# A hybrid decoder layer: two-input elementwise work of the token mixers moved from GpSimd to VectorE and ScalarE

## The chip, the cores and the metric

The kernel runs on one core of a Trainium2 chip. The metric is the device time of one execution in microseconds; the number compared is the median of several runs. Engines are named as in the profile: PE (TensorE, matmuls), PEld (its weight loads), DVE (VectorE), ACT (ScalarE), POOL (GpSimd) and SP (the queue that issues most DMAs).

## The reference, cut to what matters

One layer, 256 tokens by 1024 features, float32. All projections of the token mixers come from one product, then two mixers run side by side, and a sparse expert network follows.

```python
proj = h @ w_in                       # 1024 x 7184
xa, ga, q, k, v, go, glr, ma, mb = split(proj)
xa = causal_depthwise_conv(xa)        # 4 taps
ya = rg_lru(xa) * gelu(ga)            # a = exp(-s); h = a h + sqrt(1 - a^2) * i * x  along the tokens
log_g = log_sigmoid(glr @ w_gate + b) / 16
o  = gla(q, k, v, log_g)              # gated linear attention, 4 heads
yb = o * rsqrt(mean(o^2) + eps) * norm_g * silu(go)
y  = sigmoid(ma) * ya + sigmoid(mb) * yb
h  = layer_norm(alpha * h + y @ w_out)
h  = layer_norm(alpha * h + moe(h))   # top 4 of 32 experts: every expert's weights are read
h  = h + sigmoid(h @ w_ple_gate + b) * (p @ w_ple)
```

## The kernel before

The order of the work is written out by hand: every engine runs its instructions in the order in which the code issues them, and there is no scheduler. Two large parts follow each other.

**The mixers.** The projection is done in blocks of 128 output channels (`proj(n, b)`; for `v` blocks of tokens, `vblock`). Each block's weights, a "half" of 128x1024, come from a DMA and are split into a high and a low part so that three passes of matmuls give a nearly exact float32 product: ACT copies the high part (L268), and L269 subtracts it to get the low part. A block is 24 matmuls of 256 columns. `split` runs up to four halves ahead (`NW = 4`), in the order xa, q, k, v, ma, ga, go, mb, wo, 64 halves in all. The table `ONPOOL` says which of them have L269 on POOL; the others have it on DVE.

The list `seq` gives the order of the blocks (8 of xa, 4 of q, 4 of k, 8 of v, 8 of ma, 8 of ga, 8 of go), and the table `hooks` says which pieces of the mixers' own work are issued behind which block: the recurrence (`lru_*`), and the attention, whose decayed products are built in levels 0 to 7. For a level, `lvl_sub` makes two halves of exponents (L467, L468), `lvl_exp` takes exp of them on ACT (L471), `lvl_mul` multiplies one half by the keys and the other by the queries (L477, L478), and `lvl` multiplies them on PE ("gr" in the profile) and puts the result in place (L496, L503, L508). Levels 0 to 5 are used early; level 7's matmuls (L507) stand ahead of the second ga block, and `assemble` and `gla_out` come after them.

The blocks of `mb` come last, with a loop of engines around each (`ev_mb`): a sigmoid on ACT (L616), two DVE products (L617, L618), ACT's high part of the result (L620), DVE's low part (L621). The halves split in that loop are the later ones of mb and the first of wo. Then `y_out` multiplies by w_out.

**The experts.** All 32 experts' weights, 12.6 MB each, stream from HBM through the large buffers that the mixers give back (`Slots`, 22 tiles of 8 KB a partition; `Stream.pump` issues the next load on SP as soon as a buffer is free). Each expert is 32 matmuls up and 16 down of 512 columns at full float32. Behind them come the second norm and the gated embedding.

Of the kernel before, what the change touches and what calls it, by code (L numbers as in the profile page):

```python
# [13 lines left out]
AF = mybir.ActivationFunctionType  # L14
# [14 lines left out]
class Slots:  # L29
    """The large buffers: tiles of 8 KB a partition that change hands. keep of them stay free for takes to come."""  # L30
# [17 lines left out]
class Stream:  # L48
    """Large loads in a fixed order, each issued as soon as a buffer is free for it."""
# [24 lines left out]
    def give(self, *names, keep=0):  # L74
        """Buffers back, keep of them for takes to come."""
        self.slots.keep += keep
        for name in names:
            self.slots.free.append(self.slots.held.pop(name))
        self.pump()
# [3 lines left out]
def hybrid_layer(ctx, tc, x, p, w_in, conv_w, conv_b, lru_w_r, lru_b_r, lru_w_i, lru_b_i, lru_lambda,  # L83
# [64 lines left out]
    # buffers held at the start, and those that the mixers take later: six of the split weights, the LRU's and the GLA's  # L148
# [66 lines left out]
    # integer level masks of the scores: entry (j, i) belongs to level l when (i ^ j) >> l == 1 and i > j  # L215
# [26 lines left out]
    # ================= phase 1: token mixers =================  # L242
    # ---- exact splits of float32 operands in two parts of 12 bits, and their products in three passes
    HALVES = [(key, c) for key in PIECES for c in range(2)]
    W3, lru = {}, {}
    ONPOOL = (1, 2, 5, 6, 12, 14, 26, 32, 35, 36, 42, 47, 48, 52, 53, 54, 55, 57, 63, 65, 70)
    ahead = {"next": 0, "keep": NW}

    def w_keep():
        """Buffers kept for the halves to split next."""  # L250
        n = min(NW - len(W3), len(HALVES) - ahead["next"])
        hold(n - ahead["keep"])
        ahead["keep"] = n

    def split(m, n=1):
        """High and low parts of the halves of pieces up to half m, as far as the buffers for them go; each in n steps."""
# [22 lines left out]
    def mm3(o, l, r, ks, first=True, last=True):  # L279
        """o += sum over k of l(k).T @ r(k), each a pair (high, low): high x high, high x low, low x high."""  # L280
# [21 lines left out]
    # four blocks of channels each: first mixer's output; recurrence gate, then second mixer's output  # L302
# [13 lines left out]
    yb = rr  # L316
# [17 lines left out]
    def lru_decay():  # L334
        """4 * softplus(-lambda), the logarithm of 1 + u as 2 * artanh(u / (2 + u)); the gates' sigmoids come as (tanh + 1) / 2."""
# [29 lines left out]
    def glr():  # L365
        """Low-rank decay gate."""
# [4 lines left out]
    def decay1():  # L371
        """Logarithms of the decays (times 16) and their running sums."""
# [33 lines left out]
    # ---- the projection's blocks of 128 channels, with the mixers' work in between  # L406
    xc, QK = {}, {}

    def proj(n, b):
        """Channel-major block b of projection n: psum [128 channels, 256 tokens]."""  # L410
# [8 lines left out]
    def conv(b, o):  # L419
        t = xc[b] = aa[:, b]  # L420
        V.tensor_scalar(t, o, pc("cw", 24 + b), pc("cb", b), op0=OP.mult, op1=OP.add)
# [3 lines left out]
    def lru_gates(b):  # L425
# [6 lines left out]
        G.tensor_scalar(ix[:, b, :], ix[:, b, :], 1.0, None, op0=OP.add)  # L432
        G.tensor_tensor(ix[:, b, :], ix[:, b, :], t, op=OP.mult)
# [5 lines left out]
    def lru_sq(h):  # L439
        G.tensor_tensor(ya(h, 4), aa[:, h:h + 4], aa[:, h:h + 4], op=OP.mult)  # L440

    def lru_one(h):
        """1 - a^2 as tanh(s) * (1 + a^2) with a = exp(-s)."""
        V.scalar_tensor_tensor(rr(h, 4), ya(h, 4), 1.0, rr(h, 4), op0=OP.add, op1=OP.mult)

    def lru_sqrt(h):
        A.activation(rr(h, 4), rr(h, 4), AF.Sqrt, scale=0.25)
# [13 lines left out]
    # level lv of the decayed products: queries of the right, keys of the left half of each 2s tokens,  # L461
    # both scaled by the decay to the last token of the left half
    def lvl_sub(lv):
# [3 lines left out]
        G.tensor_tensor(half(d, 0, s), ref, half(bc, 0, s), op=OP.subtract)  # L467
# [5 lines left out]
    def lvl_mul(lv):  # L473
# [3 lines left out]
        G.tensor_tensor(half(k2, 0, s), half(d, 0, s), half(kT, 0, s), op=OP.mult)  # L477
# [50 lines left out]
    def split_bu(n):  # L528
        """Biases of the experts in three exact bfloat16 parts, stacked on the partitions."""
# [8 lines left out]
    def router_prep():  # L538
        """Norm's scale and shift folded into the router: scaled weights, their column sums, and the bias, on all partitions."""
# [17 lines left out]
    def gla_out(h):  # L557
# [6 lines left out]
        V.tensor_copy(yb(2 * h, 2), o)  # L564
        G.tensor_tensor(sqs[h], yb(2 * h, 2), yb(2 * h, 2), op=OP.mult)

    def gla_ms(h):
        """Mean squares of a head, tokens on the partitions."""
# [22 lines left out]
    def ev_q(b, o):  # L591
        V.tensor_scalar(qT[:, b, :], o, 128.0 ** -0.5, None, op0=OP.mult)

    def ev_k(b, o):
        V.tensor_copy(kT[:, b, :], o)

    def ev_ga(b, o):
        gl = tmp("gl", p1, 3)
        A.activation(gl, o, AF.Gelu_apprx_tanh)
        G.tensor_tensor(ya(b), ya(b), gl, op=OP.mult)  # L600

    def ev_go(b, o):
# [3 lines left out]
        G.tensor_tensor(yb(b), yb(b), sg, op=OP.mult)  # L606

    def ev_ma(b, o):
        sg = tmp("sg", p1, 3)
        A.activation(sg, o, AF.Tanh, scale=0.5)  # L610
        G.tensor_scalar(sg, sg, 0.5, 0.5, op0=OP.mult, op1=OP.add)
        G.tensor_tensor(ya(b), ya(b), sg, op=OP.mult)
# [24 lines left out]
    def swap(*names):  # L637
        """Buffers back, kept for as many takes to come."""
        give(*names, keep=len(names))

    # what runs after each piece, by the piece's number
# [80 lines left out]
    # ================= routing =================  # L722
# [5 lines left out]
    def ln_scale(sb, name):  # L728
        """1/std and -mean/std of the rows of both token tiles."""
# [9 lines left out]
    # residual and its transpose; the norm is applied to the logits, while the tokens are normalized beside  # L739
# [33 lines left out]
    def up_start(sel):  # L773
        """Gate and up pre-activations, tokens x d_ff: the halves of d_ff lie on the two halves of the partitions."""
# [492 lines left out]
```

## Time and profile before

| | us |
|---|---|
| median of 3 runs | 1234.04 |
| the runs | 1232.08 to 1234.21 |
| span of the profiled execution, first to last instruction | 1230.1 |
| median less span | 3.9 |

| engine | busy us in the span | share |
|---|---|---|
| PE | 1152.5 | 94% |
| DVE | 421.5 | 34% |
| ACT | 246.1 | 20% |
| POOL | 176.4 | 14% |

The profiled execution's own time is known by its span; the 3.9 us are what the runs' median has more, before the first and after the last instruction. Shares over the whole span mix the mixers (roughly the first 257 us) with the experts, in which DVE, ACT and POOL have little to do, so the sections below go by stretches. A busy PE is not PE at its peak, since the ends of matmuls are modelled.

### The profile page before, as it was taken

Reading aid. Unit: us, or ns where it says so; the run is one execution under the profiler, and the core shown is the slowest. Engines: PE = TensorE matmul, PEld = TensorE weight load, DVE = VectorE, ACT = ScalarE, POOL = GpSimd, SP = SyncE. Lnnn points to the kernel's source line nnn. Section 1 sums busy time; section 2 is a strip of 40 time slices with the busy share of each in tenths; the row PEclk is TensorE's granted clock in tenths of the full one; section 3 lists DMA queues with packets and bytes.
Section 4 is the critical chain, followed back from the end, with each engine's and each line's share of the span. In section 5 each row is a group of like instructions: output and inputs, shape, how many; then the busy total and the mean of one; then the engine's idle time right before and its main releaser. Section 6 shows DMA issues by size and latency. Waiting matters only on the chain.

```text
span 1230.1 us, 14483 instructions
## 1 busy us (share of the span) xinstructions
PE 1152.5 (94%) x5930; PEld 570.8 (46%) x5930; DVE 421.5 (34%) x680; ACT 246.1 (20%) x390; POOL 176.4 (14%) x149
## 2 busy tenths in 40 slices
PE   7998799889999999999999999899889989999987
PEld 7998799654433334333433433243234323433336
DVE  7699566731121222222121221212121212121248
ACT  4674454421111001000100100010001000200043
POOL 5757854210000000000000000000000000000025
PEclk9999899999999999899999999999999999999999
DMA  9653647588989999999999999999999999999960
GB/s 320 208 172 103 203 167 308 209 339 347 426 330 426 426 427 427 419 426 428 426 427 427 426 427 426 427 426 426 427 426 427 427 426 426 426 428 427 426 287 35
DMA packets 92715, 447.07 MB, mean 363 GB/s; under 512 B 9258, under 2 KB 40336, under 8 KB 43397
## 3 DMA queue, kind: packets, MB, share of 16 engines
q1 hardware_dynamic: 91040, 444.72, 88.2%
q10 hardware_dynamic: 1364, 1.10, 0.4%
q8 instruction: 48, 0.79, 0.2%
q0 software_dynamic: 240, 0.28, 0.1%
q14 instruction: 23, 0.18, 0.0%
HBM read 445.03 MB, written 1.05 MB: 363 GB/s over the span
## 4 chain that ended last, share of the span: by engine, by line
PE 56%; DMA 29%; DVE 7%; POOL 3%; issue 2%; ACT 2%; ACTq 0%; DVEq 0%; SPq 0%; POOLq 0%
PE gu L860 22%; DMA up<-in_w_up_dram 18%; PE dn L887 12%; DMA dn<-in_w_down_dram 11%; PE pj L283 6%; PE ga L840 4%; PE sc L920 2%; PE g L851 1%; PE acc L283 1%; PE pg L1136 1%; DVE sg L617 1%; PE gu L778 1%; DVE sgt L906 1%; PE aTp L879 1%; PE bc L929 1%
## 5 line engine op out<-in xcount | busy, mean ns | idle before, releaser
L860 PE MATMUL gu<-up,xe 128*64 128x512 f32 x1792 | 415.7, 601 | 16.6 <-DMA up<-in_w_up_dram 15.9
L860 PEld LDWEIGHTS gu<-up,xe 128*64 128x64 f32 x1792 | 121.4, 137 | 264.5 <-issue 207.4
L887 PE MATMUL dn<-dn,mo 128*64 128x512 f32 x1024 | 228.8, 597 | 5.0 <-DMA dn<-in_w_down_dram 4.8
L896 DVE COPY y2b<-dn 64x512 f32<-64x512 f32 x32 | 22.2, 694 | 379.0 <-ACT mo L898 369.2
L887 PEld LDWEIGHTS dn<-dn,mo 128*64 128x64 f32 x1024 | 73.2, 138 | 155.2 <-issue 142.1
L957 POOL DMA_DIRECT2D pp<-in_p_dram x1 | 0.8, 845 | 754.9 <-DMA up<-in_w_up_dram 754.9
L867 DVE TENSOR_SCALAR mo<-gu 128x512 f32<-128x512 f32 x32 | 22.1, 692 | 184.4 <-PE gu L860 184.4
L898 ACT ACTIVATE mo<-dn 64x512 f32<-64x512 f32 x32 | 18.9, 592 | 268.3 <-PE dn L887 268.3
L868 ACT ACTIVATE mo<-mo 128x512 f32<-128x512 f32 x32 | 20.2, 631 | 226.2 <-DVE mo L867 226.2
L860 PE MATMUL gu<-up,x 128*64 128x512 f32 x256 | 62.6, 613 | 0.0
L880 ACT ACTIVATE mo<-aTp 128x512 f32<-128x512 f32 x32 | 19.1, 598 | 206.6 <-PE aTp L879 206.6
L924 DVE TENSOR_TENSOR z<-z,sc 128x512 f32<-128x512 f32 x60 | 41.2, 688 | 48.5 <-PE sc L920 48.5
L840 PE MATMUL ga<-oh,X 128*128 128x256 f32 x224 | 55.1, 389 | 0.0
L840 PEld LDWEIGHTS ga<-oh,X 128*128 128x128 f32 x224 | 40.7, 191 | 21.4 <-DVE mo L867 5.7
L1085 POOL TENSOR_TENSOR pgl<-pg,pgh 128x1024 fp32r<-128x1024 f32 x6 | 16.3, 2748 | 175.4 <-ACT pgh L1084 171.9
L920 PE MATMUL sc<-mo,se 128*128 128x512 f32 x64 | 36.0, 645 | 0.7 <-ACT mo L898 0.7
L845 DVE TENSOR_SCALAR xe<-ga,parTB 128x256 f32<-128x256 f32 x28 | 15.2, 543 | 54.0 <-PE ga L840 54.0
L920 PE MATMUL sc<-y2b,se 128*128 128x512 f32 x64 | 32.7, 592 | 0.0
L843 ACT ACTIVATE xe<-ga,parTB 128x256 f32<-128x256 f32 x28 | 15.8, 565 | 74.8 <-PE ga L840 73.5
L879 PEld LDWEIGHTS aTp<-ident,mo 128*128 128x128 f32 x128 | 18.9, 204 | 20.8 <-issue 16.5
L860 PEld LDWEIGHTS gu<-up,x 128*64 128x64 f32 x256 | 16.3, 139 | 24.5 <-issue 22.4
L851 PEld LDWEIGHTS g<-oh,X 128*128 128x128 f32 x128 | 16.5, 193 | 18.1 <-issue 15.7
(337 smaller groups left out, 1362.9 us busy)
## 6 DMA issues: line engine op xcount, KB each, us to landing
up<-in_w_up_dram SPq DMA_DIRECT2D x256, 1024.0 KB
dn<-in_w_down_dram SPq DMA_DIRECT2D x128, 1024.0 KB
v<-in_w_in_dram SPq DMA_DIRECT2D x4, 1024.0 KB
ma<-in_w_in_dram SPq DMA_DIRECT2D x4, 1024.0 KB
ga<-in_w_in_dram SPq DMA_DIRECT2D x4, 1024.0 KB
go<-in_w_in_dram SPq DMA_DIRECT2D x4, 1024.0 KB
mb<-in_w_in_dram SPq DMA_DIRECT2D x4, 1024.0 KB
wo<-in_w_out_dram SPq DMA_DIRECT2D x4, 1024.0 KB
```

The costliest lines, as they stand in the source:

```text
L283: PE.matmul(o, lhsT=l(k)[i], rhs=r(k)[j], start=first and m == 0, stop=last and m == len(n) - 1)
L840: PE.matmul(o, lhsT=X[:, t, k * 128:(k + 1) * 128], rhs=oh[:, t], start=(t == 0), stop=(t == 1))
L851: PE.matmul(o, lhsT=X[:, t, k * 128:(k + 1) * 128], rhs=oh[:, t, i], start=(t == 0), stop=(t == 1))
L860: PE.matmul(gu[a][64 * hf:64 * hf + 64, :], lhsT=xk, rhs=w[:, (a - parts[0]) * 1024 + hf * 512:(a - parts[0]) * 1024 + hf * 512 + 512], st ...
L867: V.tensor_scalar(gc, gu[0], LIM, None, op0=OP.min)
L868: A.activation(sg, gc, AF.Sigmoid, scale=1.702)
L879: PE.transpose(o[:, q, :], act[:, c * 256 + j:(c + 1) * 256:2], ident)
L880: A.activation(aT, o, AF.Copy)
L887: PE.matmul(o[64 * dh:64 * dh + 64, :], lhsT=aT[:, 2 * c + j, hf * 64:hf * 64 + 64], rhs=w[:, j - js[0], dh * 512:(dh + 1) * 512], start=( ...
L896: V.tensor_copy(dst, src)
L920: PE.matmul(o, lhsT=se[rows, t * 128:(t + 1) * 128], rhs=(y2b if dh else mo[:, 3])[rows], start=True, stop=True)
L924: V.tensor_tensor(z[:, t, dh * 512:(dh + 1) * 512], z[:, t, dh * 512:(dh + 1) * 512], o, op=OP.add)
```

## The change

Nearly all of POOL's two-input work in the mixers goes to DVE or ACT. The table `ONPOOL` keeps two early halves; products that took two instructions on POOL become one `scalar_tensor_tensor` on DVE; squares, the evictions of q, k and of the attention's output, and the first tap of the convolution go to ACT. The factor 0.5 that `ev_ma` drops is taken up by the scale of `lru_sqrt`. The changed file has blank lines in place of comments, and some of its line numbers are lower by one.

```diff
-    ONPOOL = (1, 2, 5, 6, 12, 14, 26, 32, 35, 36, 42, 47, 48, 52, 53, 54, 55, 57, 63, 65, 70)
+    ONPOOL = (1, 2)
...
     def conv(b, o):
         t = xc[b] = aa[:, b]
-        V.tensor_scalar(t, o, pc("cw", 24 + b), pc("cb", b), op0=OP.mult, op1=OP.add)
+        A.activation(t, o, AF.Identity, scale=pc("cw", 24 + b), bias=pc("cb", b))
...
-        G.tensor_scalar(ix[:, b, :], ix[:, b, :], 1.0, None, op0=OP.add)
-        G.tensor_tensor(ix[:, b, :], ix[:, b, :], t, op=OP.mult)
+        V.scalar_tensor_tensor(ix[:, b, :], ix[:, b, :], 1.0, t, op0=OP.add, op1=OP.mult)
...
     def lru_sq(h):
-        G.tensor_tensor(ya(h, 4), aa[:, h:h + 4], aa[:, h:h + 4], op=OP.mult)
+        A.activation(ya(h, 4), aa[:, h:h + 4], AF.Square)
...
-        A.activation(rr(h, 4), rr(h, 4), AF.Sqrt, scale=0.25)
+        A.activation(rr(h, 4), rr(h, 4), AF.Sqrt, scale=0.0625)
...
-        G.tensor_tensor(half(d, 0, s), ref, half(bc, 0, s), op=OP.subtract)
+        V.tensor_tensor(half(d, 0, s), ref, half(bc, 0, s), op=OP.subtract)
...
-        G.tensor_tensor(half(k2, 0, s), half(d, 0, s), half(kT, 0, s), op=OP.mult)
+        V.tensor_tensor(half(k2, 0, s), half(d, 0, s), half(kT, 0, s), op=OP.mult)
...
-        V.tensor_copy(yb(2 * h, 2), o)
-        G.tensor_tensor(sqs[h], yb(2 * h, 2), yb(2 * h, 2), op=OP.mult)
+        A.activation(sqs[h], o, AF.Square)
+        A.activation(yb(2 * h, 2), o, AF.Copy)
...
     def ev_q(b, o):
-        V.tensor_scalar(qT[:, b, :], o, 128.0 ** -0.5, None, op0=OP.mult)
+        A.activation(qT[:, b, :], o, AF.Copy, scale=128.0 ** -0.5)
 
     def ev_k(b, o):
-        V.tensor_copy(kT[:, b, :], o)
+        A.activation(kT[:, b, :], o, AF.Copy)
...
         A.activation(gl, o, AF.Gelu_apprx_tanh)
-        G.tensor_tensor(ya(b), ya(b), gl, op=OP.mult)
+        V.tensor_tensor(ya(b), ya(b), gl, op=OP.mult)
...
         V.tensor_tensor(sg, sg, o, op=OP.mult)
-        G.tensor_tensor(yb(b), yb(b), sg, op=OP.mult)
+        V.tensor_tensor(yb(b), yb(b), sg, op=OP.mult)
...
         A.activation(sg, o, AF.Tanh, scale=0.5)
-        G.tensor_scalar(sg, sg, 0.5, 0.5, op0=OP.mult, op1=OP.add)
-        G.tensor_tensor(ya(b), ya(b), sg, op=OP.mult)
+        V.scalar_tensor_tensor(ya(b), sg, 1.0, ya(b), op0=OP.add, op1=OP.mult)
```

Three places in the queues. First DVE in the v blocks, from the exponents of level 1 to the split of the last v half: "y" and "aa" belong to the recurrence, "gd", "gc", "gq" and "gk" to the levels. Before:

```order
L468 TENSOR_TENSOR gd<-gc 128x256x2
L490 TENSOR_TENSOR gc<-gr,eye_96 128x512
L450 TENSOR_TENSOR y_210<-y_210,ix 128x1024
L454 SCALAR_TENSOR_TENSOR y_210<-aa,y_210 128x256 x4
L450 TENSOR_TENSOR y_211<-y_211,ix 128x1024
L478 TENSOR_TENSOR gq<-gd,gk 128x512
L478 TENSOR_TENSOR gq<-gd,gk 128x256x2
L269 TENSOR_TENSOR v_1047<-v_505,v_1047 128x1024
L269 TENSOR_TENSOR v_1050<-v_505,v_1050 128x1024
```

And with the change:

```order
L467 TENSOR_TENSOR gd<-gc 128x256x2
L468 TENSOR_TENSOR gd<-gc 128x256x2
L490 TENSOR_TENSOR gc<-gr,eye_96 128x512
L450 TENSOR_TENSOR y_210<-y_210,ix 128x1024
L454 SCALAR_TENSOR_TENSOR y_210<-aa,y_210 128x256 x4
L450 TENSOR_TENSOR y_211<-y_211,ix 128x1024
L477 TENSOR_TENSOR gq<-gd,gk 128x512
L478 TENSOR_TENSOR gq<-gd,gk 128x512
L477 TENSOR_TENSOR gq<-gd,gk 128x256x2
L478 TENSOR_TENSOR gq<-gd,gk 128x256x2
L269 TENSOR_TENSOR v_1039<-v_502,v_1039 128x1024
L269 TENSOR_TENSOR v_1042<-v_502,v_1042 128x1024
```

Each level's L467 and L477, which stood in POOL's queue, now stand in DVE's, so both halves of a level are done one after the other.

Second, ACT between the k blocks and the v blocks (L592 and L595 are the evictions of q and k, L439 is the square that was POOL's). Before, from the split of the second k half:

```order
L268 ACTIVATE k_676<-k_140 128x1024
L268 ACTIVATE k_707<-k_205 128x1024
L436 ACTIVATE aa<-y_210,nlam 128x256
L437 ACTIVATE y_210<-y_210,lamc 128x256
L436 ACTIVATE aa<-y_210,nlam 128x256
L437 ACTIVATE y_210<-y_210,lamc 128x256
L268 ACTIVATE k_741<-k_205 128x1024
```

And with the change:

```order
L268 ACTIVATE k_669<-k_140 128x1024
L592 ACTIVATE gk<-pj 128x256
L268 ACTIVATE k_700<-k_205 128x1024
L592 ACTIVATE gk<-pj 128x256
L435 ACTIVATE aa<-y_210,nlam 128x256
L436 ACTIVATE y_210<-y_210,lamc 128x256
L435 ACTIVATE aa<-y_210,nlam 128x256
L436 ACTIVATE y_210<-y_210,lamc 128x256
L439 ACTIVATE y_210<-aa 128x1024
L268 ACTIVATE k_734<-k_205 128x1024
```

Evictions and the square now stand between the high parts that PE and DVE wait for.

Third, DVE around the mb blocks. Before, two blocks in a row, whose splits are on POOL:

```order
L617 TENSOR_TENSOR sg<-sg,y_210 128x256
L618 TENSOR_TENSOR sg<-sg,y_210 128x256
L621 TENSOR_TENSOR yhl<-sg,yhl 128x256
L617 TENSOR_TENSOR sg<-sg,y_210 128x256
L618 TENSOR_TENSOR sg<-sg,y_210 128x256
L621 TENSOR_TENSOR yhl<-sg,yhl 128x256
```

And with the change:

```order
L616 TENSOR_TENSOR sg<-sg,y_210 128x256
L617 TENSOR_TENSOR sg<-sg,y_210 128x256
L620 TENSOR_TENSOR yhl<-sg,yhl 128x256
L269 TENSOR_TENSOR mb_2255<-mb_1620,mb_2255 128x1024
L616 TENSOR_TENSOR sg<-sg,y_210 128x256
L617 TENSOR_TENSOR sg<-sg,y_210 128x256
L620 TENSOR_TENSOR yhl<-sg,yhl 128x256
```

The split of the half that is to come stands in DVE's queue ahead of the block's own products.

## Rows read from the trace of the kernel before

**Rows 1.** Busy time (and instructions) of each engine by stretch, clock, DMA share.

```profile
95.00:111.00 16.00, 14.43 (x199) 13.86 (x195) 15.90 (x17) 5.37 (x8) 10.54 (x7) 0.91 0.25 72
111.00:141.00 30.00, 23.11 (x237) 22.64 (x237) 23.03 (x17) 15.77 (x22) 29.26 (x24) 0.96 0.65 199
141.00:150.00 9.00, 9.00 (x66) 8.88 (x65) 4.22 (x4) 2.91 (x4) 5.87 (x4) 0.74 0.32 92
150.00:204.00 54.00, 54.00 (x430) 53.08 (x428) 31.33 (x40) 28.48 (x37) 31.75 (x24) 1.00 0.68 260
266.00:380.00 114.00, 113.11 (x544) 48.28 (x544) 25.66 (x59) 15.99 (x32) 0.00 (x0) 0.99 0.90 361
380.00:669.00 289.00, 282.79 (x1241) 103.14 (x1242) 69.79 (x125) 26.41 (x46) 0.00 (x0) 0.98 1.01 426
669.00:1173.00 504.00, 473.63 (x2040) 168.53 (x2036) 103.33 (x183) 48.22 (x84) 0.84 (x1) 0.99 1.01 427
```

**Rows 2.** The chain that ended last, one piece from the experts.

```profile
669.23 19.48 DMA up<-in_w_up_dram
```

**Rows 3.** Timeline of mb blocks: start, us, engine, line, [idle before <-releaser].

```profile
219.22 2.39 POOL L269 TENSOR_TENSOR mb<-mb,mb 128x1024 fp32r<-128x1024 f32 x1 [2.21 <-ACT mb L268]
219.44 2.44 DVE L617 TENSOR_TENSOR sg<-sg,y 128x256 f32<-128x256 f32 x1 [0.79 <-ACT sg L616]
...
222.71 1.04 ACT L268 ACTIVATE mb<-mb 128x1024 fp32r<-128x1024 f32 x1
...
227.31 1.04 ACT L268 ACTIVATE wo<-wo 128x1024 fp32r<-128x1024 f32 x1
...
228.39 1.23 DVE L269 TENSOR_TENSOR wo<-wo,wo 128x1024 fp32r<-128x1024 f32 x1 [0.52 <-ACT wo L268]
...
229.53 0.42 DVE L617 TENSOR_TENSOR sg<-sg,y 128x256 f32<-128x256 f32 x1
...
230.76 1.05 ACT L268 ACTIVATE wo<-wo 128x1024 fp32r<-128x1024 f32 x1
```

**Rows 4.** PE in the timeline of the v, ma and first ga blocks.

```profile
94.57 3.56 PE L484 MATMUL gr<-gq 128*64 128x64 f32 x64 [2.83 <-DVE gq L478]
...
140.60 1.97 PE L501 MATMUL gr<-gq 128*64 128x64 f32 x16 [6.89 <-POOL gq L477]
...
142.50 2.08 PE L283 MATMUL pj<-xh,ga 128*128 128x256 f32 x8
...
146.84 1.05 PE L507 MATMUL gr<-gq 128*128 128x128 f32 x8
...
147.65 1.20 PE L283 MATMUL pj<-xh,ga 128*128 128x256 f32 x8
```

**Rows 5.** DVE in the same stretch, timeline.

```profile
92.62 1.20 DVE L450 TENSOR_TENSOR y<-y,ix 128x1024 f32<-128x1024 f32 x1
93.74 1.28 DVE L478 TENSOR_TENSOR gq<-gd,gk 128x512 f32<-128x512 f32 x2
94.94 4.04 DVE L269 TENSOR_TENSOR v<-v,v 128x1024 fp32r<-128x1024 f32 x2
...
100.11 3.47 DVE L454 TENSOR_TENSOR_SCAN y<-aa,y 128x256 f32<-128x256 f32 x4
...
129.76 0.74 DVE L496 COPY_PREDICATED gc<-mk,gr 128x512 f32<-128x512 int32 x1
```

**Rows 6.** Groups of DVE and ACT instructions: busy us, mean ns | idle before, releaser.

```profile
L586 DVE SCALAR_TENSOR_TENSOR y<-y,parTB,ri 128x256 f32<-128x256 f32 x8 | 3.6, 476 | 0.5 <-POOL y L606 0.5
...
L604 ACT ACTIVATE sg<-pj 128x256 f32<-128x256 f32 x8 | 3.1, 382 | 8.1 <-PE pj L283 8.1
...
L748 ACT ACTIVATE nT<-tn 128x512 f32<-128x512 f32 x4 | 2.1, 602 | 10.3 <-PE tn L747 10.3
L447 ACT ACT_TABLE_LOAD x1 | 1.3, 1283 | 0.0
```

**Rows 7.** ACT's high part of a v half, timeline.

```profile
72.79 1.06 ACT L268 ACTIVATE v<-v 128x1024 fp32r<-128x1024 f32 x1 [1.50 <-DMA bd<-in_b_down_dram]
```

## Prediction

> **What bounds the kernel now.** Read the stretches first. From 266 us on the experts run: the DMA share is 0.90 up to 380 and 1.01 to 1173, at 426 to 427 GB/s [rows 1], and in the second half of it the chain of waits goes through weight loads, 19.48 us in one piece [rows 2]. PE is close behind with 282.79 of 289 us. The volume is fixed and, once saturated, the DMA can't be hurried; but it only becomes saturated when buffers come free, and those are held by the mixers. So the end moves with the end of the mixers, almost us for us, and nothing that the change does after 266 us matters, since POOL is at 0.00 there already.
>
> In the mixers the stretches say where time can be had. From 150 to 204 PE has 54.00 of 54.00 and 430 matmuls, about 0.126 us each, so a block of 24 takes 3.0 us; nothing is to be won. It loses time in two places. In 95 to 141 DVE has 15.90 of 16 us busy and then POOL 29.26 of 30 [rows 1]: PE waits 2.83 us for a product of DVE and 6.89 us for one of POOL, and comes out of the second with the granted clock at 0.74 over 141 to 150, so that the first ga block takes from 142.50 to 146.84 where 3.0 is normal, and the second one starts at 147.65 [rows 4]. The other place is the loop around the mb blocks. There L617, a product of 0.42 us, takes 2.44 when a POOL split of 2.39 has begun 0.22 us before it, and ends with that split [rows 3]. With a split on POOL the loop goes round in 4.60 us (ACT's L268 at 222.71 and 227.31); with the split on DVE in 3.45 (227.31 to 230.76) [rows 3]. PE needs 3.0, so the loop is the bound there, in both.
>
> What the row of L617 shows is a wait as long as POOL's instruction. The Trainium skill (SBUF, State Buffer, section Who interferes with whom) says that a VectorE instruction with two SBUF inputs and a GpSimd instruction that reads SBUF exclude each other for a whole instruction. By that rule DVE gets its short durations wherever POOL falls silent, and the trace of the loop agrees (0.42 against 2.44); whether it holds under a full DVE queue no row here shows.
>
> **The change, part by part.**
>
> *The mb loop.* Of the seven halves split there, five are on POOL now (52 to 55 and 57 of the table), two on DVE. All five cycles become the kind that the trace shows with a split on DVE: 5 x (4.60 - 3.45) = **5.75 us**. Lower bound 4, if a cycle is lost to PE's own pace at the start; upper bound 5 x (4.60 - 3.0) = 8, if PE's pace alone were left.
>
> *xa, q, k and the start of v.* Here DVE loses the first tap and eight evictions and gets fused products and splits; PE's early waits are about 2 us, and I let them go, because ACT becomes the late one. Ahead of the v half whose high part starts at 72.79 [rows 7] ACT now has seven evictions at 0.38 [rows 6] and two squares as long as its other 1024-column passes, 1.05 [rows 3]: 4.8 us more. I choose that 1 us of it falls into idle time of its queue: the half is ready at 72.79 + 3.8 + 1.06 = 77.6. Behind it come a table load of 1.28, two square roots of 1.05, two evictions of 0.38 and two high parts of 1.05 [rows 3, 6], which gives 83.8, and DVE's split of the last, 1.23, ends at **85.0**. PE comes to about the same place as now. The eight taps on ACT cost nothing in time, since ACT waits for PE there and its queue has gaps; if it had none, they would add 8 x 0.4 = 3 us to PE's start, and this is a bound.
>
> *From there to level 7's last product DVE is the bound.* I add up what stands in its queue from the exponents of level 1 (the first row of the second order listing) to L478 of level 7, at durations that rows show without a collision: 13 splits at 1.23 [rows 3] = 16.0; 30 halves of levels, one product with the mask and one copy, 32 at 0.64 (1.28 for two) = 20.5; two products of 1.20 = 2.4; eight scans at 0.87 (3.47 for four) = 6.9; six predicated copies at 0.74 = 4.4 [rows 5]; eight fused products of ma at 0.48 [rows 6] = 3.8. Sum 54.0 us. With 1 us for waits on ACT (the exponents of level 4 stand ahead of two high parts there) it ends at 85.0 + 55.0 = 140.0. PE's ga block 1 can then start 0.9 us later (146.84 to 147.65 now), at 140.9. The product of level 6, which PE needs before ga block 0, lies 4.4 us ahead (a split, a fused product, a predicated copy, a copy and the two halves of level 7), at 135.6. PE will have waited 1 to 3 us for it. If the clock falls as it does now, 1.9 for the matmuls and 4.34 for the block [rows 4] bring ga block 1 to 142.7. Between 140.9 and 142.7 I take the middle, 141.8, against 147.65: **5.8 us**. Bounds: no waits at all would take away 2.83 and 6.89 and about 2.3 us of low clock, 12; and if the collisions stayed in DVE's durations, see the rivals, it loses 16.
>
> *ga and go, 141 to 204.* DVE has 31.33 of 54 us [rows 1]; it gets 16 products of 0.42 and five splits of 1.23 [rows 3], 12.9 us more at most, and ACT, with 28.48, gets eight passes of 0.60 for squares and evictions [rows 6], 4.8. Both stay below PE's 54, so they cost **0**. Without that cover the products would add their 0.42 to each block, 7 us. POOL's own time, once free, is waited for by nobody in the mixers.
>
> *The sum.* 5.75 + 5.8 = 11.55 us off the span of 1230.1, 1218.5; the runs lie 3.9 above the span, so **1222.4 us**, 11.6 below the median of 1234.04. Passing on: the DMA's idle share before 380 is what shrinks, and its buffers come free in the same order, 11.6 us sooner.
>
> **The rivals.**
>
> *PE stops waiting altogether.* Both waits, the low clock and the loop at PE's pace: 12 + 8 = 20 us, **1214**. For it: DVE's idle time in 111 to 141 (23.03 of 30 busy, collisions included). Against it: DVE's order is fixed, and level 6 and 7's products stand behind everything else.
>
> *VectorE becomes the bound and the kernel slower.* The place is the same queue of 54 us. If the splits keep the durations that they have beside POOL's work, 4.04 for two [rows 5], 13 x 0.79 = 10.3 us are added, and 32 halves grown in the same proportion add 32 x 0.37 = 11.8: 22 us later, so ga block 1 starts at about 164, 16 us late. Less 5.75 in the mb loop, that gives **1244**. It decides from the point where the sum of 54 grows by 11.6 us, 21%; from there on the mb loop pays only for the loss. The Trainium skill (Perfetto Trace Analysis, section Optimizing Scalar/DVE Operations) speaks for this: when VectorE is saturated, moving work off it, to ScalarE or even GpSimd, may help, and this change does the reverse in a stretch where DVE is at 15.90 of 16. By that rule the change loses; but the same passage warns that the two share a read port, and the trace has the 15.90 with the waits for POOL in it, so I give it little.
>
> *ACT is the later one.* If the 1 us of gaps is not there and the taps' 3 us and another 2 us of hops between engines add to it, DVE's account starts at 91, and 5.8 becomes 0: 5.75 us are left, **1228**.
>
> *It doesn't reach the end.* If the DMA is saturated over 234 to 380 anyway, an earlier end of the mixers only empties buffers sooner, and the time stays at **1234**. Against it: 0.90 over 266 to 380 [rows 1], 11 us idle of 114, behind the mixers.
>
> **How the numbers follow.** What a measurement of this kernel can tell from no change is about 0.2%, 2.5 us: 1231.5 to 1236.5. Chances: the forecast, 1217 to 1227, 0.60; PE free of waits, below 1217, 0.14; ACT or hops eat the first gain, 1227 to 1231.5, 0.11; no effect, 0.08; slower, 0.07. So faster 0.85, same 0.08, slower 0.07. The range from 1214 to 1230 leaves out about 0.04 below and 0.16 above.
>
> **What the next profile would show.** The loop: ACT's L268 every 3.45 us through the mb blocks and L616 and L617 (the old L617, L618) at 0.42 each; if not, that term is wrong. DVE's splits at 1.2 and halves at 0.64 through the v and ma blocks, DVE without idle time in about 87 to 140, and PE's two waits there ending on DVE, not POOL; the matmuls of level 7 at about 140. ACT without gaps from 50 to 85. PE still at 54 of 54 through ga and go. The DMA saturated from about 368. The forecast is wrong if DVE's sum is far from 54, if PE's start at v moves by several us through ACT, or if the experts start 11 us sooner and the end does not.

## The result and the profile after

The changed kernel takes 1211.95 us in the median (1208.49 to 1212.72, 4 runs) against 1233.06 for the kernel before in the same comparison (1230.91 to 1234.21, 4 runs). The ratio is 0.9834, with a 95% interval of 0.9815 to 0.9852: about 20 us faster. The forecast was 1222.4, in a range from 1214 to 1230, so the sign was right and the size was not: the gain is nearly twice the 11.6 us. The time is nearest to that of the rival "PE stops waiting altogether" (1214). One execution of a later kernel (the mb splits on POOL), at 1428.87 us with a granted clock of 0.77, is in a slower state of the chip and is left out of its median below. The profiled execution has a span of 1210.2 us against 1230.1.

To see where the 19.9 us of the spans came from, the same point of the program is read in both traces. The program reaches its first blocks up to 2 us earlier or later from one execution to the next, so the starts below are counted from the first matmul of the recurrence's gates (PE L428, at 29.05 us before and 28.34 after). A later table goes on with the same points for the experiments.

| PE starts, us behind the first gate matmul | before | after | won |
|---|---|---|---|
| matmuls of levels 0 and 1 | 65.5 | 61.2 | 4.3 |
| matmuls of level 6 | 111.6 | 100.5 | 11.1 |
| matmuls of level 7 | 117.8 | 104.5 | 13.3 |
| first attention output ("go") | 121.6 | 108.2 | 13.3 |
| first of the attention's norm scales ("ri"), late in go | 163.7 | 150.4 | 13.3 |
| transposes behind y_out ("tn") | 227.2 | 208.0 | 19.2 |
| from there to the end of the span | 973.8 | 973.9 | 0 |

So 13.3 us are won up to level 7, nothing in ga and go, 5.9 from mb to y_out, and all of it reaches the end. The windows of the kernel after, in the columns of [rows 1], show the stages:

```profile
82.00:103.00 21.00, 18.36 (x211) 17.71 (x208) 20.86 (x30) 10.33 (x14) 3.62 (x2) 0.97 0.31 101
103.00:118.00 15.00, 15.00 (x165) 14.57 (x165) 13.97 (x21) 9.12 (x12) 0.00 (x0) 0.93 0.54 173
118.00:128.00 10.00, 10.00 (x110) 9.80 (x112) 9.37 (x15) 5.06 (x8) 0.00 (x0) 1.00 0.82 246
128.00:134.00 6.00, 6.00 (x83) 5.93 (x82) 5.43 (x9) 4.03 (x6) 0.00 (x0) 1.00 0.53 173
134.00:190.00 56.00, 56.00 (x446) 55.08 (x446) 35.51 (x56) 34.26 (x46) 1.24 (x2) 1.00 0.75 274
190.00:222.00 32.00, 32.00 (x231) 29.78 (x229) 21.45 (x37) 16.43 (x29) 0.00 (x0) 1.00 0.51 192
246.00:360.00 114.00, 113.11 (x547) 48.61 (x546) 25.45 (x59) 15.97 (x32) 0.00 (x0) 0.99 0.89 356
360.00:649.00 289.00, 282.80 (x1242) 103.15 (x1242) 69.96 (x125) 26.38 (x46) 0.00 (x0) 0.98 1.01 427
```

From 103 us on PE is busy without a gap, up to 222. DVE is at 13.97 of 15, 9.37 of 10 and 5.43 of 6 beside it: it keeps up, but hardly. The last two rows are those of 266:380 and 380:669 in [rows 1], 20 us earlier and otherwise the same. PE's timeline over the places of [rows 4] (start, us, what, idle time before and its releaser):

```profile
89.53 2.45 PE L484 MATMUL gr<-gq 128*64 128x64 f32 x64 [0.77 <-DVE gq L478]
...
101.56 1.95 PE L283 MATMUL pj<-xh,ma 128*128 128x256 f32 x8 [1.72 <-DVE ma L269]
...
128.80 1.10 PE L501 MATMUL gr<-gq 128*64 128x64 f32 x16
129.83 1.22 PE L283 MATMUL pj<-xh,ga 128*128 128x256 f32 x8
...
132.81 1.06 PE L507 MATMUL gr<-gq 128*128 128x128 f32 x8
133.62 1.20 PE L283 MATMUL pj<-xh,ga 128*128 128x256 f32 x8
```

The wait of 6.89 us is gone, and with it the low clock behind it: ga block 0 goes from 129.83 to 132.81, 2.98 us, where it took 4.34. The 2.83 us ahead of levels 0 and 1 are 0.77. DVE in the same stretch:

```profile
79.30 2.36 DVE L269 TENSOR_TENSOR v<-v,v 128x1024 fp32r<-128x1024 f32 x2 [0.99 <-ACT v L268]
81.58 0.69 DVE L467 TENSOR_TENSOR gd<-gc 128x512 f32<-128x512 f32 x1
...
84.72 2.44 DVE L454 TENSOR_TENSOR_SCAN y<-aa,y 128x256 f32<-128x256 f32 x4
...
88.19 0.68 DVE L477 TENSOR_TENSOR gq<-gd,gk 128x512 f32<-128x512 f32 x1
88.80 0.68 DVE L478 TENSOR_TENSOR gq<-gd,gk 128x512 f32<-128x512 f32 x1
...
112.47 1.22 DVE L269 TENSOR_TENSOR ma<-ma,ma 128x1024 fp32r<-128x1024 f32 x1
113.60 0.42 DVE L611 SCALAR_TENSOR_TENSOR y<-sg,y 128x256 f32<-128x256 f32 x1
113.94 1.22 DVE L269 TENSOR_TENSOR ma<-ma,ma 128x1024 fp32r<-128x1024 f32 x1
...
127.03 0.69 DVE L478 TENSOR_TENSOR gq<-gd,gk 128x512 f32<-128x512 f32 x1
...
131.21 0.68 DVE L478 TENSOR_TENSOR gq<-gd,gk 128x512 f32<-128x512 f32 x1
```

The account that the prediction drew up runs from L467 at 81.58 (its first row) to the end of L478 at 131.21 + 0.68 = 131.89: 50.3 us, and PE takes level 7's product 0.92 us later, at 132.81. Level 6's product ends at 127.03 + 0.69 = 127.72, and PE takes it 1.1 us later, at 128.80. PE waits for neither. Read the distance from one start to the next, not only the durations: L477 takes 0.68 us, but the next instruction starts 0.61 behind it; a split takes 1.22, and the next starts after 1.13; L611 takes 0.42, the next after 0.34. Four scans take 2.44 where [rows 5] has 3.47.

In the mb loop:

```profile
198.16 1.04 ACT L268 ACTIVATE mb<-mb 128x1024 fp32r<-128x1024 f32 x1
...
200.38 0.42 DVE L616 TENSOR_TENSOR sg<-sg,y 128x256 f32<-128x256 f32 x1
...
200.84 0.42 DVE L617 TENSOR_TENSOR sg<-sg,y 128x256 f32<-128x256 f32 x1
...
201.62 1.04 ACT L268 ACTIVATE mb<-mb 128x1024 fp32r<-128x1024 f32 x1
...
222.76 13.49 PE L283 MATMUL acc<-wo,yhl 128*128 128x512 f32 x58 [0.76 <-DVE wo L269]
```

ACT's high parts lie 3.46 us apart, and both products take 0.42, as forecast. PE does its eight mb blocks in 23.1 us (189.9 to 213.0), 2.9 each, where it took 27.7 before. It meets the loop once, in y_out, and waits 0.76 us.

### The profile page after: what moved, and what is told of

It is laid out like the page before. It is cut to its first block, busy times and chain, and to the rows that moved or that the text cites. A ratio compares the mean times of both kernels' runs of the same rounds, so it can differ in the third digit from the quotient of the medians.

```text
span 1210.2 us, 14420 instructions
## 1 busy us (share of the span) xinstructions
PE 1149.1 (95%) x5930; PEld 569.8 (47%) x5930; DVE 415.3 (34%) x725; ACT 258.5 (21%) x416; POOL 51.1 (4%) x62
## 4 chain that ended last, share of the span: by engine, by line
PE 65%; DMA 25%; DVE 5%; ACT 3%; issue 1%; POOL 0%; ACTq 0%; DVEq 0%; SPq 0%; POOLq 0%
PE gu L859 25%; DMA up<-in_w_up_dram 16%; PE dn L886 13%; PE pj L283 10%; DMA dn<-in_w_down_dram 9%; PE ga L839 3%; PE sc L919 3%; PE acc L283 2%; PE g L850 1%; PE pg L1135 1%; PE gu L777 1%; DVE sgt L905 1%; PE bc L928 1%; PE aTp L878 1%; PE pl L970 1%
## 5 line engine op out<-in xcount | busy, mean ns | idle before, releaser
L866 DVE TENSOR_SCALAR mo<-gu 128x512 f32<-128x512 f32 x32 | 22.1, 692 | 185.3 <-PE gu L859 185.3
L868 DVE TENSOR_SCALAR mo<-gu 128x512 f32<-128x512 f32 x32 | 22.1, 692 | 5.3 <-PE gu L859 5.2
```

The lines of the kernel that those rows point to most:

```text
L866: V.tensor_scalar(gc, gu[0], LIM, None, op0=OP.min)
L868: V.tensor_scalar(uc, gu[1], LIM, -LIM, op0=OP.min, op1=OP.max)
```

## The experiments

The question after the result: what gave the 13.3 us ahead of ga, when the forecast had 5.8? The theory: PE is the bound from 103 us on and DVE is just ahead of it; the account of DVE's queue was too long, and what the prediction hung on its end was right. The rivals are that DVE's queue has plenty of room, or that it was the bound all along. The table has all runs, with the points of the table above; the text takes the runs in order.

| kernel | median us | ratio to before, 95% | levels 0, 1 | level 6 | "go" | "tn" |
|---|---|---|---|---|---|---|
| before | 1233.06 | | 65.5 | 111.6 | 121.6 | 227.2 |
| after | 1211.95 | 0.9834 (0.9815 to 0.9852) | 61.2 | 100.5 | 108.2 | 208.0 |
| DVE + 4.8 us | 1218.67 | 0.9888 (0.9866 to 0.9910) | 61.2 | 103.6 | 112.9 | 212.7 |
| DVE + 9.6 us | 1222.63 | 0.9928 (0.9901 to 0.9954) | 61.2 | 108.4 | 117.6 | 217.4 |
| mb splits on POOL | 1218.01 | 0.9880 (0.9852 to 0.9908) | 61.2 | 100.5 | 108.3 | 213.9 |
| early splits on POOL | 1216.33 | 0.9872 (0.9847 to 0.9896) | 65.1 | 104.8 | 113.5 | 213.3 |
| levels on POOL | 1215.72 | 0.9869 (0.9850 to 0.9889) | 63.7 | 102.6 | 110.7 | 210.4 |
| products on POOL | 1214.56 | 0.9860 (0.9836 to 0.9884) | 61.2 | 100.4 | 108.3 | 208.2 |
| ACT's part undone | 1212.41 | 0.9847 (0.9826 to 0.9869) | 61.7 | 99.8 | 107.6 | 207.4 |
| mb loop reordered | 1212.14 | 0.9843 (0.9822 to 0.9864) | 61.2 | 100.5 | 108.2 | 206.8 |
| levels and products on POOL | 1223.31 | 0.9931 (0.9912 to 0.9950) | 63.3 | 106.3 | 116.2 | 216.1 |
| before, levels on DVE | 1224.99 | 0.9941 (0.9922 to 0.9960) | 62.9 | 103.9 | 113.2 | 220.5 |
| tuned | 1207.83 | 0.9807 (0.9788 to 0.9826) | 60.3 | 97.7 | 105.5 | 204.0 |

From "tn" to the end of the span lie 973.8 to 977.1 us in all of these, so a difference at "tn" passes on us for us, within 3.3 us.

**DVE's queue made longer.** Level 6's exponents are computed five, then nine times.

```diff
-        28: [(lvl, 4), (lvl_sub, 6)],
+        28: [(lvl, 4)] + [(lvl_sub, 6)] * 5,
```

> The changed kernel with level 6's two exponent halves computed five times instead of once (same values each time): eight more DVE instructions of 0.60 us, 4.8 us, ahead of the products of levels 6 and 7. Theory (PE is the bound behind 103 us and DVE is only about 1 us ahead of it: level 7's last product ends at 131.9, PE takes it at 132.8): PE waits about 4 us for level 6's product at about 128.8, and the end comes 4 to 6 us later, 1216 to 1218. Rival (DVE was far from being a bound there, its queue has slack): within 1 us of 1212. Rival (DVE's queue was the bound all along, as the prediction had it): the full 4.8 and more, with the clock down behind the wait, 1217 to 1219.

> The same with level 6's exponents nine times: 9.6 us more DVE work, so that level 7's last product ends at about 141.5, near the 140.0 that the prediction had forecast. Theory (the forecast failed by its account of DVE's queue alone, and what follows from a late product was right): PE waits about 8.7 us, the granted clock falls behind the wait as in the kernel before, ga block 1 starts at about 143 to 145, and the time is 1221 to 1224, that is about what the prediction gave. Rival (the wait costs only its own length less the slack, no clock): 1220.5 with ga block 1 at 142.3. Rival (slack): under 1215.

With 4.8 us more the time is 1218.67, which lies in the range of the rival "bound all along" and 0.7 above the theory's; with 9.6 it is 1222.63, in the theory's. PE's wait in the first, and the timeline of the second:

```profile
132.24 1.12 PE L501 MATMUL gr<-gq 128*64 128x64 f32 x16 [2.93 <-DVE gq L478]
```

```profile
134.60 0.69 DVE L478 TENSOR_TENSOR gq<-gd,gk 128x512 f32<-128x512 f32 x1
...
135.43 1.94 PE L501 MATMUL gr<-gq 128*64 128x64 f32 x16 [7.72 <-DVE gq L478]
137.31 1.84 PE L283 MATMUL pj<-xh,ga 128*128 128x256 f32 x8
...
138.69 0.68 DVE L478 TENSOR_TENSOR gq<-gd,gk 128x512 f32<-128x512 f32 x1
...
140.90 1.06 PE L507 MATMUL gr<-gq 128*128 128x128 f32 x8
141.71 1.20 PE L283 MATMUL pj<-xh,ga 128*128 128x256 f32 x8
```

And its window behind the wait, in the columns of [rows 1]:

```profile
135.00:138.00 3.00, 2.57 (x19) 2.48 (x20) 2.91 (x5) 1.62 (x2) 0.00 (x0) 0.50 0.97 313
```

Here is a case like the one that the prediction described: DVE comes late, and the granted clock behind the wait is 0.50, the lower of its two levels (1.2 GHz). Level 7's product ends at 139.37, and ga block 1 starts at 141.71. The forecast's 140.0 and 141.8 are on the clock of the trace before, whose first gate matmul is at 29.05 and not at 27.06; counted from there, the run is 1.4 and 1.9 us later than the forecast. PE also waits 7.72 us for level 6, where the prediction had 1 to 3, because PE itself comes earlier. Against the kernel before, 4.0 us are won at "go" (forecast 5.8) and 9.8 at "tn" (forecast 11.55), so that the time of 1222.63 stands so near to the forecast's 1222.4 is in part luck. In the run with 4.8 us more, PE waits 2.93 us for level 6. In both, the delay at "go" is the wait and some 1.7 us more (4.7 = 2.93 + 1.7; 9.4 = 7.72 + 1.7), nearly all of it in the slow matmuls behind the wait. DVE's delay at level 6's product is some 1.1 us longer than PE's wait (8.85 against 7.72 in the second, against the kernel after). So DVE has 1.1 us of room there and no more. The rival of a queue with plenty of room has fallen. The rival of DVE as the bound all along gives nearly the same times and is told apart by the trace alone: without the added work PE doesn't wait there, with it it does, 1.1 us less than DVE comes later.

**The mb splits back on POOL.**

```diff
-    ONPOOL = (1, 2)
+    ONPOOL = (1, 2, 52, 53, 54, 55, 57)
```

> The changed kernel with the splits 52 to 55 and 57 back on POOL, nothing else. Theory (the loop around the mb blocks was worth 5.75 us): ACT's high parts 4.60 us apart again in five cycles, end 5 to 6.5 us later, 1217 to 1218.5; nothing moves ahead of 190 us. Rival (what was won there came from the earlier start of the mixers, since the experts' loads set the end): within 1 us of 1212. Rival (the loop has slack against PE now, because the blocks start earlier against the chain): 2 to 3 us.

1218.01. Nothing moves up to "go", and "tn" comes 5.9 us later. Its timeline:

```profile
200.96 2.40 POOL L269 TENSOR_TENSOR mb<-mb,mb 128x1024 fp32r<-128x1024 f32 x1 [2.22 <-ACT mb L268]
201.19 2.46 DVE L616 TENSOR_TENSOR sg<-sg,y 128x256 f32<-128x256 f32 x1 [0.79 <-ACT sg L615]
...
204.46 1.04 ACT L268 ACTIVATE mb<-mb 128x1024 fp32r<-128x1024 f32 x1
...
209.06 1.04 ACT L268 ACTIVATE mb<-mb 128x1024 fp32r<-128x1024 f32 x1
```

The picture of [rows 3] is back: a product of 0.42 that ends 0.3 us behind POOL's split, and a cycle of 4.60 us. This is the size of the prediction's term, 5.75, by itself. Both rivals, nothing and 2 to 3 us, have fallen.

**The early splits back on POOL.**

```diff
-    ONPOOL = (1, 2)
+    ONPOOL = (1, 2, 5, 6, 12, 14, 26, 32, 35, 36)
```

> The changed kernel with the splits 5, 6, 12, 14, 26, 32, 35 and 36 back on POOL (xa, k, ma, ga), nothing else. The levels' halves stay on DVE, and POOL has nothing else to do there. DVE gets 8 x 1.23 = 9.8 us less. Theory (the lead of 14 us at ga came from PE being fed in time, which DVE alone just does): the splits beside POOL make DVE's two-input work wait for them by turns, 2.4 us each, so that four of them between 103 and 133 cost DVE about what they save; lead at ga between 10 and 15 us, time 1211 to 1216. Rival (the splits on POOL alone were what made the early waits, the 2.4 us lead at xa among them): 2.4 us lost at the third to fifth xa block and another 2 to 4 at ma, 1216 to 1219.

1216.33, 5.3 us lost at "go". The time is in the rival's range, 0.3 above the theory's; the parts are not the rival's 2.4 and 2 to 4. 3.8 are lost by the start of the q blocks, the rest at levels 6 and 7:

```profile
32.24 2.08 PE L283 MATMUL pj<-xh,xa 128*128 128x256 f32 x8 [2.17 <-POOL xa L269]
...
120.97 3.38 POOL L269 TENSOR_TENSOR ga<-ga,ga 128x1024 fp32r<-128x1024 f32 x1 [8.60 <-ACT ga L268]
...
122.13 2.77 DVE L467 TENSOR_TENSOR gd<-gc 128x512 f32<-128x512 f32 x1
...
131.95 1.12 PE L501 MATMUL gr<-gq 128*64 128x64 f32 x16 [1.43 <-DVE gq L478]
```

One split on POOL turns an L467 of 0.68 us into 2.77 and is itself 3.38 instead of 2.4. DVE has 9.8 us less to do in this kernel, and level 6's product is 4.3 us later all the same, most of it brought along from the xa blocks.

**The levels' halves back on POOL.** In `lvl_sub` and `lvl_mul` the first of the two instructions:

```diff
-        V.tensor_tensor(half(k2, 0, s), half(d, 0, s), half(kT, 0, s), op=OP.mult)
+        G.tensor_tensor(half(k2, 0, s), half(d, 0, s), half(kT, 0, s), op=OP.mult)
```

> The changed kernel with the levels' first halves (exponents and products with the keys, 16 instructions) back on POOL, nothing else. DVE's queue gets 16 x 0.60 = 9.6 us shorter, POOL's holds little but these. Theory (each half on POOL takes 1.3 us alone and makes DVE's two-input work of that time wait; DVE was 1 us ahead of PE): level 0 and 1 come 2 to 3 us later at 89.5, as in the kernel before (2.83), and levels 6 and 7 come in time or up to 2 us late, since POOL's queue is short; 1213 to 1217. Rival (the place of these halves on POOL was the cause of the wait of 6.89 us): a wait of 4 to 7 us at level 6 again, with the clock down behind it, 1218 to 1222.

1215.72. All of the loss, 2.4 us, is made at levels 0 and 1; levels 6 and 7 come in time.

```profile
85.51 3.41 POOL L477 TENSOR_TENSOR gq<-gd,gk 128x512 f32<-128x512 f32 x2 [14.34 <-ACT gd L471]
...
85.63 5.01 DVE L454 TENSOR_TENSOR_SCAN y<-aa,y 128x256 f32<-128x256 f32 x4
...
92.50 3.11 PE L484 MATMUL gr<-gq 128*64 128x64 f32 x64 [2.83 <-DVE gq L478]
```

Four scans take 5.01 us beside two POOL products, against 2.44. In the kernel before, the same four scans, at 87.69, take 5.01 too. The wait of 2.83 in [rows 4] is explained by this: DVE was late there because of POOL. The wait of 6.89 isn't.

**The products back on POOL**: the recurrence's input product, and those of ga, go and ma, in two instructions where they were two.

```diff
-        V.scalar_tensor_tensor(ya(b), sg, 1.0, ya(b), op0=OP.add, op1=OP.mult)
+        G.tensor_scalar(sg, sg, 0.5, 0.5, op0=OP.mult, op1=OP.add)
+        G.tensor_tensor(ya(b), ya(b), sg, op=OP.mult)
```

> The changed kernel with the recurrence's input product, the products of ga, go and ma back on POOL (in two instructions where they were two), nothing else. Theory (what POOL's L477 of level 6 waited for was POOL's own queue of such products; with the halves on DVE the products on POOL are waited for by nobody, but collide with DVE's two-input work): 16 POOL instructions of ma between 110 and 133 take DVE's time by turns, DVE's queue grows by a few us against 8 x 0.33 saved, PE waits 1 to 5 us at level 6, and the 2.4 us of the xa blocks go if POOL's products stand ahead of a split there; 1213 to 1219. Rival (off the path of PE, products on POOL cost nothing): 1211 to 1213.

1214.56, but 0.1 us at "go" and 0.2 at "tn"; the rest of the difference in time arises behind "tn" (976.9 us against 973.9), within what these kernels show there. The time alone is in the theory's range, the points are the rival's. PE waits 0.91 us at level 6, just under the 1 to 5 that the theory named, and it is made up elsewhere (level 4 starts 1.1 us sooner; why isn't shown). The products cost about nothing by themselves.

**ACT's part undone**: the first tap, the evictions of q, k and the attention's output on DVE, the squares on POOL, as in the kernel before.

> The changed kernel with the first convolution tap and the evictions of q, k and the attention's output back on DVE, the squares back on POOL, nothing else. The prediction had ACT as the late engine ahead of the v blocks, 4.8 us more work for it and DVE's account starting at 85.0. Theory (ACT had room, and DVE is only 1 us ahead of PE from 103 to 133, but the moved evictions lie before 82 or after 134): the start of the v blocks moves by less than 1 us either way, DVE's queue in 82 to 133 is as it was; 1211 to 1214. Rival (ACT was the late one at v): DVE's account starts 2 to 3 us earlier and PE's waits at 89.5 and 101.6 go, 1209 to 1211. Rival (DVE before 82 was just short of being late, and the taps and evictions make it so): 2 to 4 us lost ahead of v, 1214 to 1216.

1212.41, and "tn" within 0.6 us of the kernel after. PE loses 1.2 us at the recurrence's gates of the xa blocks, where it now waits for DVE's taps, and has it back by levels 2 and 3. DVE's account now starts 52.5 us behind the first gate matmul instead of 53.2, so ACT's part had cost it 0.7 us net, not the 2 to 3 of the rival, and this part of the change is worth nothing in either direction.

**Levels and products on POOL together.** Since neither explains the 6.89 us, the two were put together.

> The changed kernel with both the levels' first halves and the products of the recurrence, ga, go and ma back on POOL; all splits but two stay on DVE. Apart, the two cost 2.4 and 0.1 us up to the first ga blocks. Theory (a queue: in the kernel before, POOL's part of level 6 stood behind ma's products, some 17 us of them, and 13 us of other halves in the same 25 us; neither alone fills POOL): together they cost more than the sum, a wait of 3 to 7 us at level 6 that ends on POOL, the clock down behind it, 7 to 11 us up to ga, 1219 to 1223. Rival (the splits on POOL filled the queue, not these): the sum of the two, 2 to 4 us, 1214 to 1216.5.

1223.31, 0.3 above the theory's range: 8.0 us lost at "go", where the two alone lose 2.4 and 0.1.

```profile
132.00 1.57 POOL L613 TENSOR_TENSOR y<-y,sg 128x256 f32<-128x256 f32 x1
133.53 1.26 POOL L478 TENSOR_TENSOR gq<-gd,gk 128x512 f32<-128x512 f32 x1
...
134.84 1.97 PE L502 MATMUL gr<-gq 128*64 128x64 f32 x16 [3.86 <-POOL gq L478]
```

POOL's part of level 6 (L478 here) starts with the end of a product of ma, without idle time ahead of it, and PE waits 3.86 us for it. The kernel before has the same picture:

```profile
138.60 0.72 POOL L612 TENSOR_TENSOR y<-y,sg 128x256 f32<-128x256 f32 x1
139.28 1.26 POOL L477 TENSOR_TENSOR gq<-gd,gk 128x512 f32<-128x512 f32 x1
```

So the wait of [rows 4] is a queue on POOL. In 111 to 141 POOL is busy for 9.64 us with the levels alone, 14.59 with the products alone, 25.45 with both, and 29.26 in the kernel before, which has splits there too. That these splits make up the rest, from 3.86 to 6.89, is not shown.

**One part alone in the kernel before**: the levels' halves on DVE.

> The kernel before with the levels' first halves on DVE, nothing else: the one part alone. Theory (they shorten POOL's queue by some 22 us of work, and the wait of 6.89 us with its low clock goes, while the splits on POOL go on colliding, and the mb loop stays): PE's wait at level 6 falls to 1 to 3 us and ends on DVE, 6 to 9 us of the 13.3 up to ga are won, nothing in the mb loop, 1223.5 to 1227. Rival (VectorE becomes the bound, as the prediction's second rival had it: the same DVE work more, with the collisions kept): the wait at level 6 stays at 5 us or more, now on DVE, 1231 or slower.

1224.99: 8.3 us won at "go" of 13.3, nothing in the mb loop, and 1.6 lost again in y_out, where the granted clock is 0.80 over 236 to 242 (1.00 at the same place of the kernel before). PE's wait at level 6 is 2.70 us and ends on DVE:

```profile
123.18 2.89 DVE L468 TENSOR_TENSOR gd<-gc 128x512 f32<-128x512 f32 x1
...
132.45 1.82 PE L501 MATMUL gr<-gq 128*64 128x64 f32 x16 [2.70 <-DVE gq L478]
```

An L468 of 2.89 beside a split of POOL shows what is left: the collisions. The rival, VectorE as a bound that makes the kernel slower, fails here too, with all of the levels on DVE and POOL still at work.

**The mb loop in another order**: a block's high and low part of the result (the last two instructions of `ev_mb`) are issued behind the next half's split.

```diff
     for b in range(8):
-        ev_mb(b, proj("mb", b))
+        o = proj("mb", b)
+        if late2:
+            ev_mb2(*late2)
+        late2 = ev_mb(b, o)
```

> The changed kernel with the mb loop in another order: a block's high part and low part of the result are issued behind the next half's split, so that ACT goes from the sigmoid to the next half's high part without waiting for DVE's two products. Theory (in the changed kernel PE is the bound through the mb blocks too, 32.0 of 32 us busy, and waits once, 0.76 us, in y_out): the cycle of ACT falls from 3.45 to about PE's 2.9, but only 0.8 us are won, 1211. Rival (the loop of 3.45 us is the bound, as the prediction had it): eight cycles by 0.5 us, 4 us won, 1208.

1212.14. ACT's high parts now lie 2.88 us apart, the wait of 0.76 us is gone, y_out runs without a gap, and "tn" comes 1.2 us sooner, less than the time can tell. Four us were not to be had: with the loop at 3.46, PE's own pace already was the bound to within 1.2 us.

**A faster version.** To the other order of the mb loop are added three moves in DVE's queue, each of which lets a product that PE waits for go ahead of one that nobody waits for yet.

```diff
-        19: [(diag,), (lru_in, 0), (lru_scan, 0), (lru_in, 4), (lvl_exp, 0), (lvl_mul, 0), (lvl_exp, 1),
-            (lvl_mul, 1)],
+        19: [(diag,), (lru_in, 0), (lru_scan, 0), (lvl_exp, 0), (lvl_mul, 0), (lvl_exp, 1),
+            (lvl_mul, 1), (lru_in, 4)],
...
-        21: [(lru_scan, 4), (lvl, 0), (lvl, 1), (lvl_mul, 2), (lvl_exp, 3)],
-        22: [(swap, "ix", "aa"), (take_FF,), (lvl_mul, 3), (lvl_sub, 4), (lvl_sub, 5)],
+        21: [(lvl, 0), (lvl, 1), (lvl_mul, 2), (lvl_exp, 3)],
+        22: [(lvl_mul, 3), (lvl_sub, 4), (lvl_sub, 5), (lru_scan, 4), (swap, "ix", "aa"), (take_FF,)],
...
-        31: [(lvl, 5), (lvl, 6), (lvl_exp, 7), (lvl_mul, 7)],
+        31: [(lvl, 5), (lvl_exp, 7), (lvl_mul, 7), (lvl, 6)],
```

> The changed kernel with the mb loop in the other order, and on DVE three pieces moved: the second input product of the recurrence behind the products of levels 0 and 1, its second four scans behind the exponents of levels 4 and 5, and level 7's products ahead of the copy of level 6. Nothing leaves an engine. Theory (PE is the bound from 103 us on, and what is left is its waits of 0.7, 0.8, 1.7 and 0.8 us ahead of or behind it): 1 to 3 us up to ga and 1.2 in y_out, span 1207 to 1209, time 1208 to 1210.5. Rival (DVE's sum up to level 7 sets ga, whatever its order, since it is only 1 us ahead): what is won at 101 us is lost again at level 6 or 7, only the 1.2 us of y_out stay, 1211.

1207.83, ratio 0.9807 (0.9788 to 0.9826): faster than the kernel before. Against the changed kernel the ratio is lower, but the two intervals just overlap, so by the times alone a gain isn't shown; by the points of the traces it wins 2.7 us at "go" and 3.9 at "tn". From its timeline:

```profile
125.02 1.12 PE L501 MATMUL gr<-gq 128*64 128x64 f32 x16 [0.56 <-DVE gq L478]
...
209.24 22.26 PE L283 MATMUL acc<-wo,yhl 128*128 128x512 f32 x96
```

A wait of 0.56 us is back at level 6: what was won earlier has used up DVE's 1.1 us of room.

## Why the prediction was wrong in size

**Right.** That the collisions with POOL go at both places, the size of the mb loop's term (5.75 forecast, 5.9 measured and 5.9 by its own experiment), the zero for ga and go, and the passing on to the end, us for us. The products at 0.42 and the splits at 1.2 on DVE came as described. In the mb term there is some luck: its premise, that the loop at 3.45 us stays the bound, held only in y_out, and a faster loop wins 1.2 us more, not four.

**The step that failed** is "From there to level 7's last product DVE is the bound", by its account: start at 85.0, 54.0 + 1 us, end at 140.0. Measured: 81.6, 50.3, 131.9. That is 8.1 us, and at this pace not DVE but PE is the bound, since PE waits for neither level 6 nor level 7. The 8.1 us are nearly the whole error at the first ga block (13.3 won instead of 5.8, with 0.7 us between the two profiles' starts). They have two halves, and PE's own arrival stands beside them.

*The start, 3.4 us.* The prediction let PE's early waits go, "because ACT becomes the late one". The run with ACT's part undone shows that ACT's part costs the start of the account 0.7 us net, and PE nothing from levels 2 and 3 on. The lead was kept: the q blocks begin 1.7 us sooner behind the first gate matmul, 2.4 us on the clock of the trace. ACT's work did reach the v half of [rows 7]:

```profile
73.41 1.06 ACT L268 ACTIVATE v<-v 128x1024 fp32r<-128x1024 f32 x1 [0.70 <-DMA bd<-in_ln_b_dram]
```

It starts at 73.41 instead of 72.79. Counted from the first gate matmul that is 1.3 us later, for 4.8 us more work, where the prediction had 3.8; the earlier start and the gaps in ACT's queue, of which the prediction counted 1 us, took the rest.

*The length, 4.7 us.* Every duration was read from a row, and each row was longer than what the instruction costs in a full queue. By the distances between starts above, 32 halves at 0.60 are 19.2 us (20.5 in the account), 13 splits at 1.13 are 14.7 (16.0), eight fused products at 0.34 are 2.7 (3.8). The eight scans cost 4.7 (6.9), since the row in [rows 5], "without a collision" as the prediction put it, did have one. One of POOL's products ran beside its scans:

```profile
100.84 1.61 POOL L477 TENSOR_TENSOR gq<-gd,gk 128x512 f32<-128x512 f32 x1 [2.94 <-ACT gd L471]
```

Together that is 5.9 us too much, and 0.7 too little for idle time (1.7 us where 1 was allowed), 5.2 in all, of which 4.7 show; the other 0.5 us are small gaps that no term names. The Trainium skill (Perfetto Trace Analysis, section Optimizing Scalar/DVE Operations) says in a bracket that a profiled latency holds a part that overlaps with the next instruction; the trace agrees, with 0.08 to 0.09 us for each of these instructions.

*PE's arrival, 4.2 us.* The prediction had PE come "to about the same place as now". In the kernel before PE stands ready for level 6 at 140.60 - 6.89 = 133.71, 104.7 us behind the first gate matmul; in the kernel after it takes it at 100.5. The 13.3 us are these 4.2, the wait of 6.89, and 2.2 that level 6 and ga block 0 take less at the higher clock. A shorter account alone, with PE at its old pace, would by these rows have won 9.1.

With the account's end 8 us earlier, level 6's product came ahead of PE, and then the terms that hung on its lateness went too: no wait, no low clock. The experiment with 9.6 us more DVE work puts the account's end back to within 1.4 us of the forecast's, and 9.8 us are then won up to "tn" where the forecast had 11.55. So the steps behind the account, a wait for DVE and the low clock behind it, were right in kind; the length of the wait was not, since PE comes earlier.

**The rivals.** PE without its large waits came true, at a chance of 0.14, but its sum of 12 + 8 us is met by other parts, 13.3 + 5.9, which is in part luck. It needed no loop at PE's pace, since PE reached y_out before the loop could hold it up by more than 0.76 us, so the words "the loop is the bound there, in both" hold for the kernel before alone. VectorE as the bound stays 1.1 us away, DVE's room at level 6. The sum of that rival has a slip: 0.79 on the 1.23 of a split is 0.41 on a half's 0.64, not 0.37, so its 11.8 us are 13.2 and its time is 1.4 us longer. The run with the levels on POOL takes 9.6 us off DVE's queue and is 2.4 us later at "go". The rule of the Trainium skill (Perfetto Trace Analysis, section Optimizing Scalar/DVE Operations) that such a move may help a saturated VectorE, GpSimd included, doesn't hold here; its warning about the shared port does. The Trainium skill (SBUF — State Buffer, section Who interferes with whom) names who is hit: a VectorE instruction with two SBUF inputs beside a GpSimd one that reads SBUF. The trace agrees under a full queue too: 2.77 for 0.68 beside a split, and scans doubled.

## What to carry to other kernels

Where an engine's queue decides, add up distances between the starts of back-to-back instructions, not their durations, and take them from a place where the engine that collides with it is silent; here this was 6 us of 54. Then set the end of the sum beside the time at which the consumer would come by its own pace, since on the near side of that point the whole chain of waits and low clock behind it vanishes at once. And price edits together: two parts that cost 2.4 and 0.1 us alone cost 8.0 together, because only both fill a queue.

## What the runs showed that was not expected

A wait of 2.93 us and one of 7.72 us ahead of the same matmuls cost the same 1.7 us more, nearly all of it for the clock behind them. The cost doesn't follow the wait's length in the other runs either: from the start of level 6 to that of level 7 PE takes 4.0 us in the kernel after, 5.5 behind waits of 2.70, 2.93 and 7.72 us, and 6.2 behind waits of 3.86 and 6.89. And POOL pays for a collision too: its split takes 3.38 us beside DVE's two-input work, against 2.40 in the mb loop.
